# Token-major products that read each block of weights as two alternating streams

## The chip, the cores and the metric

The kernel runs on one core of one Trainium2 chip. The metric is the device time of one execution in microseconds; the weights are laid out on the host before the launch, which is not part of it.

## The reference

One layer of a decoder on 256 tokens with 2048 features, all in float32: a feed-forward block, a mixer of two gated branches, and a second feed-forward block, each followed by a layer norm over a scaled residual. Cut to what matters:

```python
h = layer_norm(DN_ALPHA * h + 0.5 * swiglu(h, ffn1_w_in[l], ffn1_w_out[l]), ln1_g[l], ln1_b[l])
q, k, v, qi, ki, wi, rx, rg, gates = split_cols(h @ w_in[l])
y_attn = dsa_attention(q, k, v, qi, ki, wi)
y_rnn = rglru_branch(rx, rg, conv_w[l], ...)
g_attn, g_rnn = jnp.split(jax.nn.sigmoid(gates), 2, axis=-1)
merged = g_attn * (y_attn @ w_attn_branch[l]) + g_rnn * (y_rnn @ w_rnn_branch[l])
h = layer_norm(DN_ALPHA * h + merged @ w_out[l], ln2_g[l], ln2_b[l])
h = layer_norm(DN_ALPHA * h + 0.5 * swiglu(h, ffn2_w_in[l], ffn2_w_out[l]), ln3_g[l], ln3_b[l])
```

`swiglu` is `(silu(a) * b) @ w_out` with `a, b` the halves of `h @ w_in`; its inner width is 5632. The weights are some 520 MB that are read once, and nearly all of the arithmetic is in products of the 256 tokens with them.

## The kernel before

**Products in three parts.** TensorE multiplies in a rounded float32 format (`float32r`). To keep precision, every operand is split into a rounded part h and a remainder l, and a product is three matmuls: h·h, h·l and l·h. For weights the split is done on the chip, piece by piece: ACT writes h (line 294, `hl`), then DVE writes l = w - h (line 295). A piece has up to 1024 columns; five split pieces can be held at a time (`HL_BUFS = 5`), and the class `Weights` loads and splits a few pieces ahead of the one in use. Some pieces of the feed-forward's second matrix are split by ACT and a DMA that adds (tiles `wd`).

**Token-major products.** In most products the activations are the stationary operand (128 features by 128 tokens, loaded by each matmul) and the weights are the moving one, in runs of 512 or 256 columns; the result lies in PSUM with tokens on partitions. These go through `three` (lines 766, 767 and 768, one for each part) and, at the start of a block behind a norm, through lines 793 and 795 in `eager`. The 512-column form is used for plain blocks of weights (`tokens`), the 256-column form for fast products: for some blocks seven products of 2 by 2 sub-blocks take the place of eight. They need sums of weight blocks, which DVE makes (`operand`, lines 249 to 256, each on blocks of 256 columns), and which are then split like other pieces.

**Feature-major products.** The recurrent branch and the index keys use weights as the stationary operand and 256 tokens as the moving one (`mm3`, lines 1415 to 1417; `mmB`, lines 756 and 757). They are not touched.

**Order.** PE, SP and POOL run in the order in which the code is written. The order of the work is set by a list of pieces and by plans written out by hand; ACT and DVE are ordered by a scheduler. In the time of the profile, the first feed-forward block runs to about 650 us, the mixer to about 1620, and the second feed-forward block from there to the end.

**Layout on the host.** `_layout` puts every weight matrix into blocks as the kernel loads them: `f_in` and `f_out` for the feed-forward, `a_blocks` for all other token-major products, `b_blocks` for the feature-major ones.

Of the kernel before, what the change touches and what calls it, by code (L numbers as in the profile page):

```python
# [15 lines left out]
P = 128  # L16
S = 256
D = 2048
FF = 5632
NK = D // P  # L20
NKF = FF // P
NBK = NKF // 2
# [366 lines left out]
def tile_layer(ctx, tc, x_fm, x_tm, pos, f1a, f1o, wA, wki, wB, wG, lru, wab, wrb, wo, f2a, f2o,  # L389
# [6 lines left out]
    V, A, T, G = nc.vector, nc.scalar, nc.tensor, nc.gpsimd  # L396
# [21 lines left out]
    def MM():  # L418
        return psum.tile([P, 512], F32, name=name("mm"), tag="mm", bufs=4)
# [65 lines left out]
    for i in range(NR + LAG):  # L485
# [4 lines left out]
        if i >= LAG:  # L490
            g, c = divmod(i - LAG, TPG)
            o = sum(LRU_COLS[:c])
# [266 lines left out]
    def blockB(x):  # L759
# [2 lines left out]
            mmB(ps, x[k], W.unit(P), k == 0, k == len(x) - 1)  # L762
        return ps

    def three(ps, xh, xl, w, start, stop):
        T.matmul(ps, xh, w[0], start=start, stop=False)  # L766
        T.matmul(ps, xh, w[1], start=False, stop=False)  # L767
        T.matmul(ps, xl, w[0], start=False, stop=stop)  # L768

    def tokens(ps, x, t, w, start, stop):  # L770
        three(ps, x[:, 0, t * P:(t + 1) * P], x[:, 1, t * P:(t + 1) * P], w, start, stop)

    def eager(hs, ps):


        ln, hs.halves = hs.halves, None
        behind = ln.behind
        base = W.cur + 1
        W.limit, W.cap = base + AHEAD - 1, len(W.pieces)
        with tc.issue_after(ln.normed):  # L780
            W.split_to(W.limit)
        ws = []
        for k in range(0, 8, 2):
            if k == 2:
                with tc.issue_after(behind[0]), tc.issue_after(behind[1]):
                    W.split_to(base + AHEAD)
            if k == 6:
                ln.half(1)
            ws += [W.unit(512) for _ in range(2)]
            for a in range(2):  # L790
                for j in (k, k + 1):
                    x = ln.first[j][:, a, :P]
                    T.matmul(ps[0], x, ws[j][0], start=j == 0 and a == 0, stop=False)
                    if a == 0:
                        T.matmul(ps[0], x, ws[j][1], start=False, stop=False)
        for k in range(8):
            tokens(ps[1], hs[k], 1, ws[k], k == 0, False)
            if k % 2:
                W.split_to(base + AHEAD + 1 + k // 2)
        W.limit = None  # L800

    def blockF(x, forms, plan, fill):
# [10 lines left out]
        if getattr(x, "halves", None):  # L813
            c = [MM(), MM()]
            eager(x, c)
            skip = 4
        for i, (form, k) in enumerate(plan):
# [26 lines left out]
            def run(ps, ops, start, stop):  # L844
                for r in range(2):
                    three(ps, *ops[r], W.unit(S), start and r == 0, stop and r == 1)
# [14 lines left out]
    def blockA(x, finish=None, lag=0, ln=None):  # L861
# [10 lines left out]
        if getattr(x, "halves", None):  # L872
            eager(x, ps)
            k = 8
# [677 lines left out]
    for j in range(-1, NR + LAG):  # L1552
# [15 lines left out]
        if j >= LAG:  # L1568
            i = j - LAG
            g, c = divmod(i, TPG)  # L1570
            xg = xcs[g * TPG:(g + 1) * TPG] if c else None
            if c == 1:
                open_heads = [BP() for _ in range(4)]
                ws = [W.unit(P) for _ in range(2)]
                for m in range(2):
                    for wi_, xi in ((0, 0), (0, 1), (1, 0)):
                        for b in range(4):
                            rows = slice(b * TAIL, (b + 1) * TAIL)
                            T.matmul(open_heads[b][:, m * S:(m + 1) * S], ws[m][wi_][rows], xg[0][rows, xi],
                                     start=m == 0 and wi_ == 0 and xi == 0, stop=False)  # L1580
            if c:
                ps = open_heads[c - 1]
# [3 lines left out]
            if c == TPG - 1:  # L1586
                ps = MM()
# [31 lines left out]
    for nb in range(4):  # L1619
# [3 lines left out]
        g, a = got  # L1623
# [19 lines left out]
def _layout(x, positions, ffn1_w_in, ffn1_w_out, ln1_g, ln1_b, w_in, conv_w, conv_b, lru_wa, lru_ba,  # L1643
            lru_wx, lru_bx, lru_lambda, w_attn_branch, w_rnn_branch, w_out, ln2_g, ln2_b, ffn2_w_in,
            ffn2_w_out, ln3_g, ln3_b):
    import numpy as np

    def c(a):
        return np.ascontiguousarray(a)

    def f_in(w):
        return c(w.reshape(NK, P, 2, NBK, 256).transpose(3, 1, 0, 2, 4)).reshape(NBK, P, NK * 512)

    def f_out(w):
        return c(w.reshape(NKF, P, 4, 512).transpose(2, 1, 0, 3)).reshape(4, P, NKF * 512)

    def a_blocks(w):
        n = w.shape[1] // 512
        nk = w.shape[0] // P
        return c(w.reshape(nk, P, n, 512).transpose(2, 1, 0, 3)).reshape(n, P, nk * 512)  # L1660

    def b_blocks(w):
        nk, n = w.shape[0] // P, w.shape[1] // P
        v = w.reshape(nk, P, n, P).transpose(2, 0, 1, 3).reshape(nk * n // 16, 16, P, P)
        return c(v.transpose(0, 2, 1, 3)).reshape(nk * n // 16, P, 2048)

    order = np.concatenate([np.concatenate([g * 640 + n * 160 + np.arange(HEAD, HEAD + TAIL) for n in range(4)]
                                           + [g * 640 + n * 160 + np.arange(HEAD) for n in range(4)])
                            for g in range(GRP)])
    w = w_in[0]  # L1670
    rx, rg = w[:, 4176:6736][:, order], w[:, 6736:9296][:, order]
    ki = np.zeros((D, P), w.dtype)
    ki[:, :80] = w[:, 4096:4176]

    lr = []
    for g in range(GRP):
        both = [[wm[g * 4 + n] for n in range(4)] for wm in (lru_wa[0], lru_wx[0])]
        u = [np.concatenate([wm[n][HEAD:, :HEAD] for n in range(4)], 0) for wm in both]
        for n in range(4):
            u += [wm[n][:HEAD, :HEAD] for wm in both]  # L1680
        for wm in both:
            tail = np.zeros((TPG, P, P), w.dtype)
            for n in range(4):
                c0 = n * TAIL
                tail[0, c0:c0 + TAIL, c0:c0 + TAIL] = wm[n][HEAD:, HEAD:]
                tail[1 + n, :, c0:c0 + TAIL] = wm[n][:HEAD, HEAD:]
            u += list(tail)
        lr.append(np.stack(u, 1).reshape(P, -1))

    def pc(vec, n):  # L1690
        return vec.reshape(n, P).T

    cols = np.concatenate([pc(ln1_g[0], NK), pc(ln1_b[0], NK), pc(ln2_g[0], NK), pc(ln2_b[0], NK)]
                          + [pc(conv_w[0, k][order], NR) for k in range(4)]
                          + [pc(a[0][order], NR) for a in (conv_b, lru_ba, lru_bx, lru_lambda)], axis=1)
    return dict(
        x_fm=c(x[0].reshape(S, NK, P).transpose(2, 1, 0)).reshape(P, NK * S), x_tm=c(x[0]),
        pos=c(positions[0].reshape(2, P).T),
        f1a=f_in(ffn1_w_in[0]), f1o=f_out(ffn1_w_out[0]), wA=a_blocks(w[:, :4096]),
        wki=c(ki.reshape(NK, P, P).transpose(1, 0, 2)).reshape(P, 2048), wB=b_blocks(np.concatenate([rx, rg], 1)),  # L1700
        wG=a_blocks(w[:, 9296:]),
        lru=c(np.stack(lr)), wab=a_blocks(w_attn_branch[0]), wrb=a_blocks(w_rnn_branch[0][order]),
        wo=a_blocks(w_out[0]), f2a=f_in(ffn2_w_in[0]), f2o=f_out(ffn2_w_out[0]), cols_d=c(cols),
        ln1_g=c(ln1_g[0]), ln1_b=c(ln1_b[0]), ln2_g=c(ln2_g[0]), ln2_b=c(ln2_b[0]),
        ln3_g=c(ln3_g[0]), ln3_b=c(ln3_b[0]))
# [16 lines left out]
```

## Time and profile before

| | us |
|---|---|
| median of 3 runs | 2339.02 (2338.2 to 2341.13) |
| span of the profiled execution, first to last instruction | 2334.1 |
| PE busy | 2309.5 |
| DVE busy | 2180.3 |
| ACT busy | 1583.6 |
| POOL busy | 304.6 |

The profile gives the execution's span and not its time with what lies around it; the median of the runs is 4.9 us above the span. Matmul records overlap, since a matmul is pipelined with the next: the spacing of their starts is what a matmul costs, not the length of its record. `PEld` is the load of the stationary operand, which runs beside PE. A row of the timeline gives start, length, engine, line, operation, output tile <- input tiles, shapes and count; where a row has a count over one, its length is from the first start to the last end. DMA moves 559.57 MB at a mean of 240 GB/s, and the granted TensorE clock is 0.999 of full speed over the span.

### The profile page before, as it was taken

Reading aid. Unit: us, or ns where it says so; the run is one execution under the profiler, and the core shown is the slowest. Engines: PE = TensorE matmul, PEld = TensorE weight load, DVE = VectorE, ACT = ScalarE, POOL = GpSimd, SP = SyncE. Lnnn points to the kernel's source line nnn. Section 1 sums busy time; section 2 is a strip of 40 time slices with the busy share of each in tenths; the row PEclk is TensorE's granted clock in tenths of the full one; section 3 lists DMA queues with packets and bytes.
Section 4 is the critical chain, followed back from the end, with each engine's and each line's share of the span. In section 5 each row is a group of like instructions: output and inputs, shape, how many; then the busy total and the mean of one; then the engine's idle time right before and its main releaser. Section 6 shows DMA issues by size and latency. Waiting matters only on the chain.

```text
span 2334.1 us, 40566 instructions
## 1 busy us (share of the span) xinstructions
PE 2309.5 (99%) x15430; PEld 2109.1 (90%) x15430; DVE 2180.3 (93%) x3172; ACT 1583.6 (68%) x2345; POOL 304.6 (13%) x416
## 2 busy tenths in 40 slices
PE   8999999999999999999999999999999999999998
PEld 7899999999988999888899998888889999999997
DVE  7899999999999999879887888998999999999997
ACT  7667777777757656556557785555667777777763
POOL 1111222222210000000110001100111112222220
PEclk9999999999999999999999999999999999999999
DMA  9778899999976555554665558755787899999986
GB/s 337 242 218 261 267 269 269 275 275 269 265 230 211 187 192 211 186 189 154 244 239 194 199 184 324 241 199 191 242 272 223 258 271 275 275 266 272 268 232 212
DMA packets 149091, 559.57 MB, mean 240 GB/s; under 512 B 17408, under 2 KB 18048, under 8 KB 124448
## 3 DMA queue, kind: packets, MB, share of 16 engines
q1 hardware_dynamic: 100800, 455.00, 54.4%
q0 software_dynamic: 47952, 101.85, 21.1%
q8 instruction: 121, 1.98, 0.3%
q14 instruction: 74, 0.61, 0.1%
q10 hardware_dynamic: 144, 0.13, 0.0%
HBM read 519.69 MB, written 37.22 MB: 239 GB/s over the span
## 4 chain that ended last, share of the span: by engine, by line
PE 71%; DVE 19%; issue 4%; DMA 4%; ACT 2%; POOL 0%; SPq 0%; ACTq 0%; DVEq 0%; POOLq 0%
PE mm L766 15%; PE mm L767 15%; PE mm L768 15%; DVE hl L295 10%; PE bp L767 5%; PE bp L766 5%; PE bp L768 5%; PE mm L1415 2%; PE mm L1417 2%; PE mm L1416 2%; DVE ws L249 2%; ACT hl L294 2%; DVE rf L256 1%; DVE rf L253 1%; DMA raw<-f1o 1%
## 5 line engine op out<-in xcount | busy, mean ns | idle before, releaser
L294 ACT ACTIVATE hl<-rf 128x1024 fp32r<-128x1024 f32 x573 | 516.0, 913 | 292.4 <-PE mm L768 135.1
L295 DVE TENSOR_TENSOR hl<-rf,hl 128x1024 fp32r<-128x1024 f32 x573 | 593.6, 1041 | 13.4 <-ACT hl L294 11.3
L295 DVE TENSOR_TENSOR hl<-raw,hl 128x1024 fp32r<-128x1024 f32 (+2 forms) x378 | 445.8, 1192 | 64.5 <-ACT hl L294 63.4
L294 ACT ACTIVATE hl<-raw 128x1024 fp32r<-128x1024 f32 (+2 forms) x378 | 386.0, 1034 | 174.5 <-PE mm L768 84.5
L767 PE MATMUL bp<-hl,sh 128*128 128x256 f32 x1146 | 321.4, 280 | 2.8 <-DVE hl L295 2.8
L766 PE MATMUL bp<-hl,sh 128*128 128x256 f32 x1146 | 321.1, 280 | 0.0
L768 PE MATMUL bp<-hl,sl 128*128 128x256 f32 x1146 | 320.4, 280 | 0.0
L766 PE MATMUL mm<-hl,hs 128*128 128x512 f32 (+1 forms) x800 | 274.4, 343 | 3.6 <-ACT yd L1197 3.0
L767 PE MATMUL mm<-hl,hs 128*128 128x512 f32 (+1 forms) x800 | 268.4, 335 | 0.7 <-DVE hl L295 0.7
L768 PE MATMUL mm<-hl,hs 128*128 128x512 f32 (+1 forms) x800 | 267.9, 335 | 0.1
L295 DVE TENSOR_TENSOR hl<-ws,hl 128x1024 fp32r<-128x1024 f32 x191 | 233.1, 1220 | 10.1 <-ACT hl L294 10.0
L249 DVE TENSOR_TENSOR ws<-rf 128x1024 f32<-128x1024 f32 x191 | 233.4, 1222 | 8.6 <-DMA rf<-wrb 2.7
L294 ACT ACTIVATE hl<-ws 128x1024 fp32r<-128x1024 f32 x191 | 201.9, 1057 | 57.6 <-DVE ws L249 23.5
L767 PEld LDWEIGHTS bp<-hl,sh 128*128 128x128 f32 x1146 | 215.2, 188 | 5.9 <-DVE hl L295 4.6
L768 PEld LDWEIGHTS bp<-hl,sl 128*128 128x128 f32 x1146 | 218.2, 190 | 0.0
L766 PEld LDWEIGHTS bp<-hl,sh 128*128 128x128 f32 x1146 | 215.2, 188 | 1.3
L1415 PE MATMUL mm<-hs,hl 128*128 128x256 f32 x640 | 178.1, 278 | 0.0
L1417 PE MATMUL mm<-hs,hl 128*128 128x256 f32 x640 | 177.6, 278 | 0.0
L1416 PE MATMUL mm<-hs,hl 128*128 128x256 f32 x640 | 177.6, 277 | 0.0
L766 PEld LDWEIGHTS mm<-hl,hs 128*128 128x128 f32 x800 | 150.3, 188 | 21.0 <-ACT yd L1197 4.2
L768 PEld LDWEIGHTS mm<-hl,hs 128*128 128x128 f32 x800 | 151.1, 189 | 16.8 <-DVE hs L960 0.5
L767 PEld LDWEIGHTS mm<-hl,hs 128*128 128x128 f32 x800 | 150.4, 188 | 15.5 <-DVE hl L295 1.4
(360 smaller groups left out, 5994.3 us busy)
## 6 DMA issues: line engine op xcount, KB each, us to landing
rf<-f1a SPq DMA_DIRECT2D x75, 1024.0 KB, 7.5
rf<-f2a SPq DMA_DIRECT2D x75, 1024.0 KB, 6.9
raw<-f1o SPq DMA_DIRECT2D x88, 512.0 KB, 6.8
raw<-f2o SPq DMA_DIRECT2D x88, 512.0 KB, 6.7
raw<-wB SPq DMA_DIRECT2D x80, 512.0 KB, 4.7
raw<-wG SPq DMA_DIRECT2D x54, 512.0 KB, 4.4
wd<-f1o POOLq DMA_DIRECT2D x92, 256.0 KB, 9.1
wd<-f2o POOLq DMA_DIRECT2D x92, 256.0 KB, 8.7
```

The costliest lines, as they stand in the source:

```text
L249: v.tensor_tensor(t, b[:, 0:4:3], b[:, 1:2].to_broadcast([P, 2, 2, 256]), op=OP.add)
L253: v.tensor_tensor(b[:, 1], t[:, 1], b[:, 0], op=OP.add)
L256: v.tensor_tensor(b[:, 0], b[:, 1], b[:, 2], op=OP.add)
L294: nc.scalar.activation(hp, src, AF.Copy)
L295: self.last = nc.vector.tensor_tensor(lp, src, hp, op=OP.subtract)
L766: T.matmul(ps, xh, w[0], start=start, stop=False)
L767: T.matmul(ps, xh, w[1], start=False, stop=False)
L768: T.matmul(ps, xl, w[0], start=False, stop=stop)
L1415: T.matmul(ps[:, :S], w[0], x[:, 0], start=first, stop=False)
L1416: T.matmul(ps[:, :S], w[0], x[:, 1], start=False, stop=False)
L1417: T.matmul(ps[:, :S], w[1], x[:, 0], start=False, stop=last)
```

## The change

The host lays out each 256 columns of the token-major weights as the 128 even columns and then the 128 odd ones (`woven` in `_layout`). In the kernel, the moving operand of each token-major matmul is read by an access pattern that undoes this: it takes one column from the first half of the 256, one from the second half, and so on, the two 512 bytes apart. The result is written to PSUM in the order of the original columns, contiguously. With 512 columns, the pattern does one block of 256 after the other. The number and order of the instructions on every engine, the tiles and the DMAs are the same as before; on PE a few waits on its own semaphore are placed otherwise.

```diff
+    def woven(ps, w):
+
+        if ps.shape[1] == S:
+            return ps.rearrange("p (k e) -> p k e", e=2), w.rearrange("p (e k) -> p k e", e=2)
+        return (ps.rearrange("p (h k e) -> p h k e", h=2, e=2),
+                w.rearrange("p (h e k) -> p h k e", h=2, e=2))
+
+    def product_of(ps, x, w, start, stop):
+        o, m = woven(ps, w)
+        T.matmul(o, x, m, start=start, stop=stop)
+
     def three(ps, xh, xl, w, start, stop):
-        T.matmul(ps, xh, w[0], start=start, stop=False)
-        T.matmul(ps, xh, w[1], start=False, stop=False)
-        T.matmul(ps, xl, w[0], start=False, stop=stop)
+        product_of(ps, xh, w[0], start, False)
+        product_of(ps, xh, w[1], False, False)
+        product_of(ps, xl, w[0], False, stop)
...
                     x = ln.first[j][:, a, :P]
-                    T.matmul(ps[0], x, ws[j][0], start=j == 0 and a == 0, stop=False)
+                    product_of(ps[0], x, ws[j][0], j == 0 and a == 0, False)
                     if a == 0:
-                        T.matmul(ps[0], x, ws[j][1], start=False, stop=False)
+                        product_of(ps[0], x, ws[j][1], False, False)
...
+    def woven(w):
+        return w.reshape(w.shape[0], -1, P, 2).swapaxes(2, 3).reshape(w.shape)
+
     def f_in(w):
-        return c(w.reshape(NK, P, 2, NBK, 256).transpose(3, 1, 0, 2, 4)).reshape(NBK, P, NK * 512)
+        return c(woven(w).reshape(NK, P, 2, NBK, 256).transpose(3, 1, 0, 2, 4)).reshape(NBK, P, NK * 512)
...
```

`f_out` and `a_blocks` call `woven` in the same way; `b_blocks` does not.

More of the change, by code (lines that the diff above doesn't have):

```diff
@@ L1649, in c @@
         return np.ascontiguousarray(a)
+    def woven(w):
+        return w.reshape(w.shape[0], -1, P, 2).swapaxes(2, 3).reshape(w.shape)
     def f_in(w):
-        return c(w.reshape(NK, P, 2, NBK, 256).transpose(3, 1, 0, 2, 4)).reshape(NBK, P, NK * 512)
+        return c(woven(w).reshape(NK, P, 2, NBK, 256).transpose(3, 1, 0, 2, 4)).reshape(NBK, P, NK * 512)
     def f_out(w):
-        return c(w.reshape(NKF, P, 4, 512).transpose(2, 1, 0, 3)).reshape(4, P, NKF * 512)
+        return c(woven(w).reshape(NKF, P, 4, 512).transpose(2, 1, 0, 3)).reshape(4, P, NKF * 512)
     def a_blocks(w):
@@ L1659, in a_blocks @@
         nk = w.shape[0] // P
-        return c(w.reshape(nk, P, n, 512).transpose(2, 1, 0, 3)).reshape(n, P, nk * 512)
+        return c(woven(w).reshape(nk, P, n, 512).transpose(2, 1, 0, 3)).reshape(n, P, nk * 512)
     def b_blocks(w):
```

## The prediction

> **What bounds the kernel now.** I read the page's busy shares and the chain that ended last first, then what PE waited for, then the spacing of single matmuls in the timeline, and last the busy time of each engine by stage. The page:
>
> ```profile
> span 2334.1 us, 40566 instructions
> PE 2309.5 (99%) x15430; PEld 2109.1 (90%) x15430; DVE 2180.3 (93%) x3172; ACT 1583.6 (68%) x2345; POOL 304.6 (13%) x416
> PE 71%; DVE 19%; issue 4%; DMA 4%; ACT 2%; POOL 0%; SPq 0%; ACTq 0%; DVEq 0%; POOLq 0%
> ```
>
> PE is busy nearly all the time, DVE not far behind. A busy PE says little, since matmul records overlap, so the second view is what PE waited for, longest first, the first and the last of its ten rows:
>
> ```profile
> PE mm L766 <- ACT hl L294: 5.6, 1, 5.6
> PE bp L767 <- DVE hl L295: 3.7, 9, 0.9
> ...
> PE bp L951 <- DVE y L971: 0.2, 1, 0.2
> ```
>
> No row is over 5.6 us, so ten rows are under 40 us of 2334 (they add to 19). The kernel is a stream of matmuls that hardly pauses; the time is the number of matmuls times their spacing. [...] In the timeline of PE, first the three-product groups (h·h, h·l, l·h: lines 766 to 768) on 512 columns, then on 256 columns, then the feature-major products of line 1415 to 1417, which also read 256 columns and load a new stationary tile each time:
>
> ```profile
> 319.74 0.39 PE L766 MATMUL mm<-hl,g 128*128 128x512 f32 x1
> ...
> 322.24 0.39 PE L768 MATMUL mm<-hl,g 128*128 128x512 f32 x1
> 1200.23 0.28 PE L766 MATMUL mm<-hl,ya 128*128 128x256 f32 x1
> ...
> 1201.53 0.28 PE L768 MATMUL bp<-hl,sl 128*128 128x256 f32 x1
> 1259.95 0.28 PE L1417 MATMUL mm<-hs,hl 128*128 128x256 f32 x1
> ...
> 1261.54 0.28 PE L1416 MATMUL mm<-hs,hl 128*128 128x256 f32 x1
> ```
>
> There are 11 steps between the first two rows: 2.50 / 11 = 0.227 us for 512 columns. Between the next two, 11 steps: 1.30 / 11 = 0.118 us for 256 columns. Between the last two, 14 steps: 1.59 / 14 = 0.1136 us for 256 columns. So equal shapes run at two spacings, 0.118 and 0.1136, and 512 columns cost a little less than two times 256. What could the array do if its operand came without a hitch? The nearest rows are products and transposes in plain float32:
>
> ```profile
> 1018.60 0.59 PE L1406 MATMUL bp<-pT,stg 128*128 128x256 f32 x2
> L1406 PE MATMUL bp<-pT,stg x32: 377/377/382, 1018.6 to 1096.3; 128*128 128x256 f32 x32
> 46.77 0.60 PE L1174 MATMUL bp<-ident,z 128*128 128x128 f32 x4
> L1174 PE MATMUL bp<-ident,z x176: 270/272/329, 46.8 to 2293.2; 128*128 128x128 f32 x176
> ```
>
> Two records of 0.377 in 0.59 start 0.59 - 0.377 = 0.213 us apart for 256 columns; four of 0.272 in 0.60 start (0.60 - 0.272) / 3 = 0.109 us apart for 128 columns. Both are 0.83 to 0.85 ns a column, twice 0.42. If a column can be taken in half that time, as the 0.227 suggests, that is about 0.216 us for 512 columns (the mean of 2 x 0.109 and 0.213) and 0.109 for 256. The products of interest take 0.227 and 0.118: 11 and 9 ns each that the array doesn't need. I find that excess only where 4-byte columns are taken at the higher rate, so it points at the read of the moving operand, alone or against the weight load that runs beside it. This is the stretch that the change touches.
>
> **The change, part by part.** Nothing is added or removed on any engine: instruction order, tiles, bytes and semaphores stay; each weight element lies elsewhere within its 256 columns, and the moving operand of the token-major products steps half a block (512 bytes) between one column and the next. PSUM is still written column by column. The sums that feed the fast products (L249, L253, L256) and the splits (L294, L295) act element by element on blocks of 256, so they cost the same. The DMAs move the same bytes in the same pieces: nothing. An access pattern with more dimensions needn't cost: on DVE a split from a tile read in separate runs and one read in one run take the same:
>
> ```profile
> L295 DVE TENSOR_TENSOR hl<-rf,hl 128x1024 fp32r<-128x1024 f32 x382 | 464.9, 1219 | 13.1 <-ACT hl L294 11.1
> L295 DVE TENSOR_TENSOR hl<-raw,hl 128x1024 fp32r<-128x1024 f32 x361 | 436.2, 1220 | 61.0 <-ACT hl L294 60.1
> ```
>
> What is left is the spacing of the token-major products, which no row of this trace shows with an alternating read: all moving operands here are contiguous. I bound it from both sides. From below: 0.216 and 0.109 us, as above. From above: a column every two cycles, 0.213 for 256 columns as L1406 does it, and 0.426 for 512. Between these I take 0.216 for 512 columns and 0.1136 for 256. The reason is the pair of rows at 0.118 and 0.1136: same shape, same loads, yet the one pays 4 ns more. So part of the excess depends on where the operands lie, not on the amount of work, and a read that spends twice as long on each address range (two streams share the time) can shift it. For 256 columns I don't go below 0.1136 as the likely value: no product of this kind runs faster in the trace.
>
> How many, and where? One of the three lines stands for each of them, as each has 4178 matmuls; the table is line 767 by stage, with its busy time and count, then all engines in the same stages:
>
> ```profile
> core 0: us, PE busy (x) PEld busy (x), PEclk, DMA share, GB/s
> 0.00:100.00 100.00, 56.63 (x158) 30.20 (x158) 1.00 0.88 303
> 100.00:650.00 550.00, 383.61 (x1257) 235.93 (x1256) 1.00 0.88 260
> 650.00:950.00 300.00, 140.93 (x444) 83.48 (x444) 1.00 0.60 207
> 950.00:1200.00 250.00, 137.20 (x399) 74.76 (x398) 1.00 0.57 197
> 1200.00:1370.00 170.00, 1.40 (x5) 0.82 (x5) 1.00 0.62 205
> 1370.00:1620.00 250.00, 143.59 (x408) 76.79 (x409) 1.00 0.67 235
> 1620.00:1710.00 90.00, 46.58 (x129) 24.05 (x128) 1.00 0.76 247
> 1710.00:2270.00 560.00, 392.09 (x1285) 241.24 (x1285) 1.00 0.89 260
> 2270.00:2334.00 64.00, 33.35 (x97) 18.21 (x97) 0.98 0.62 206
> sum 2334.00, PE 1335.40 PEld 785.48; mean PE 148.38 PEld 87.28
> core 0: us, PE busy (x) PEld busy (x) DVE busy (x) ACT busy (x) POOL busy (x), PEclk, DMA share, GB/s
> 0.00:100.00 100.00, 94.10 (x485) 80.08 (x486) 82.07 (x130) 68.57 (x106) 11.90 (x39) 1.00 0.88 303
> 100.00:650.00 550.00, 544.69 (x3843) 508.40 (x3842) 542.06 (x659) 410.78 (x593) 109.16 (x124) 1.00 0.88 260
> 650.00:950.00 300.00, 298.58 (x2084) 275.15 (x2083) 291.17 (x562) 182.54 (x269) 10.54 (x18) 1.00 0.60 207
> 950.00:1200.00 250.00, 250.00 (x1412) 217.35 (x1410) 219.02 (x376) 147.10 (x235) 13.97 (x26) 1.00 0.57 197
> 1370.00:1620.00 250.00, 249.53 (x1381) 217.71 (x1380) 231.89 (x346) 142.97 (x188) 19.79 (x37) 1.00 0.67 235
> 1620.00:1710.00 90.00, 87.67 (x451) 73.70 (x450) 81.71 (x146) 60.80 (x111) 12.85 (x21) 1.00 0.76 247
> 1710.00:2270.00 560.00, 556.81 (x3931) 519.40 (x3930) 554.10 (x673) 418.58 (x604) 111.74 (x128) 1.00 0.89 260
> 2270.00:2334.00 64.00, 58.08 (x308) 48.37 (x306) 47.94 (x69) 24.48 (x31) 10.36 (x17) 0.98 0.62 206
> ```
>
> Busy over count is the mean record, and with 0.39 us for 512 columns and 0.28 for 256 it gives the mix: in 100 to 650 us 383.61 / 1257 = 0.305, so 77% have 256 columns. Times three lines: 3771 products, about 840 wide and 2930 narrow. What PE offers there is 840 x 11 ns + 2930 x 4 ns = 9 + 12 = 21 us. But DVE, the third busy column, is free for only 550 - 542.1 = 7.9 us in this stage, and PE's weights come from its splits: it cannot deliver them sooner than it can work. I take the smaller of offer and room in each stage:
>
> - 0 to 100: offer 4, room 18: 4.
> - 100 to 650: offer 21, room 7.9: 7.9.
> - 650 to 950 (67% narrow): offer 8.4, room 8.8: 8.4.
> - 950 to 1200 (42%): offer 9.6, room 31: 9.6.
> - 1200 to 1370 has 5 of these products a line: 0.
> - 1370 to 1620 (35%): offer 10.5, room 18: 10.5.
> - 1620 to 1710: offer 3.5, room 8.3: 3.5.
> - 1710 to 2270 (78%): offer 21, room 5.9: 5.9.
> - 2270 on (42%): offer 2.3, room 16: 2.3.
>
> The offer is 81 us, of which 52 arrive. The profiled span of 2334.1 becomes 2282; the median of the runs, 2339.0, lies 4.9 above the span, and I leave that as it is: 2287 us. What is late next is the DVE split in the two feed-forward stages. With the lower bounds (11 and 9 ns) the same sum gives about 60 us: 2279. DVE's room may be too small, as its records overlap: two adjacent splits start closer together than one lasts. If half the rest of the offer in the two feed-forward stages then got through, some 25 us more: about 2255.
>
> **The rivals.** *The read gets slower.* If the operand's reader keeps one short line of SBUF and serves two or more neighbouring columns from it, alternating streams would miss on every column. The trace neither shows nor excludes it, because every moving operand is contiguous. Its price by the L1406 rows is a column every two cycles: 0.426 - 0.227 = 0.199 us on a wide product and 0.213 - 0.118 = 0.095 on a narrow one. Over all stages the mix is 1335.4 / 4178 = 0.320, 64% narrow: 8020 narrow and 4510 wide, so 762 + 897 = 1660 us, all on the path since PE is the bound: about 4000 us. It decides as soon as a product becomes slower at all: 1 ns more on each of 12,534 is 12.5 us. For it speaks that the excess of today shows a reader without slack at the full rate; against it that contiguous columns already pay, so the reader is not simply a line that is reused. [...]
>
> *Nothing changes.* The excess could belong to the weight load or to its handover: each product loads 128 columns, and 0.1136 against 0.118 may be a matter of the stationary operand's address, which stays. Then 2339. For it: 256-column products at 0.1136 exist with a contiguous read; against it: the wide products, whose load fills only half their time, have 11 ns too.
>
> *PE speeds up and the rest doesn't follow at all*: DVE and ACT wait for each other in rings of five buffers, and a smaller share arrives: with half of 52, 2313. That is within the first case.
>
> **How the numbers follow.** Faster as worked out: 0.67, at 2287, its own range 2250 to 2330. No change in the spacing: 0.13, at 2339. Slower read: 0.20, nearly all of it far out near 4000. The range of 2250 to 2345 holds the first two and leaves out the third. A change of 0.2% (4.7 us) is about what can be told from none here, and with it the chances are 0.67, 0.13 and 0.20.
>
> **What would show it.** Right: 512-column products of the three lines start 0.216 us apart and narrow ones 0.114 or less; DVE's busy share rises to 95%, its part of the chain that ended last grows, and PE's waits for the split at L295 in the feed-forward stages grow from a few us to tens. Lines 1415 to 1417 and 1200 to 1370 us stay as they are. Wrong: an unchanged 0.227; or 0.43, with DVE and ACT half idle. It would also be wrong if PE got faster and DMA, 0.88 busy in the feed-forward stages, then kept the splits waiting.

## The result and the profile after

The changed kernel takes 2317.34 us (median of 4 runs, 2313.93 to 2322.61) against 2338.61 before (2338.04 to 2341.13): a ratio of 0.9911, 95% interval 0.9896 to 0.9925. It is faster by 21 us, where 52 were forecast. The page after, in the rows shown of before:

```profile
span 2315.4 us, 40575 instructions
PE 2242.9 (97%) x15430; PEld 2081.5 (90%) x15430; DVE 2177.0 (94%) x3172; ACT 1577.1 (68%) x2345; POOL 307.3 (13%) x416
DVE 41%; PE 30%; issue 12%; DMA 8%; ACT 7%; POOL 1%; SPq 0%; ACTq 0%; DVEq 0%; POOLq 0%
```

PE's part of the chain that ended last fell from 71% to 30%, and DVE's rose from 19% to 41%: the bound has moved. All three lines of the product are now one line, 774. Its spacing in the timeline: 12 narrow products from the first row below to the second, then 21 wide ones in one row.

```profile
314.12 0.39 PE L774 MATMUL bp<-hl,sh 128*128 128x256 f32 x2
...
315.46 0.28 PE L774 MATMUL mm<-hl,xs 128*128 128x256 f32 x1
1373.64 4.70 PE L774 MATMUL mm<-hl,hs 128*128 128x512 f32 x21
```

Narrow: 1.34 / 12 = 0.112 us instead of 0.118. Wide: the row lasts 4.70 with a record of 0.38 at its end, (4.70 - 0.38) / 20 = 0.216 us instead of 0.227. So the read did what was forecast, to the nanosecond for the wide products and a little more for the narrow ones. Over the kernel, the narrow spacing of before had a median of 0.117, so PE's offer is 4512 x 11 ns + 8070 x 5.3 ns = 92 us. The span lost 18.7. What took the rest? PE's busy time fell by 67 us, but its idle time rose from 25 to 73 (span less busy time). PE's waits, longest first, before 5.6 and 3.7 us at the head:

```profile
PE mm L774 <- DVE hl L295: 25.5, 41, 1.9
PE mm L774 <- DVE z L1173: 9.6, 6, 3.2
PE bp L774 <- DVE hl L295: 8.3, 15, 0.9
```

The two layer norms inside the kernel are good landmarks, as their transposes (line 951 before, 962 after) are PE's first work behind the first feed-forward and its last before the second. First and last start of these, and of the last matmuls of the kernel, before and then after:

```profile
L951 PE MATMUL bp<-ident,y x32: 270/272/331, 703.1 to 1628.6; 128*128 128x128 f32 x32
L1052 PE MATMUL bp<-y,dg x6: 379/592/697, 2326.3 to 2328.4; 128*128 128x512 f32 x4, 128*128 128x256 f32 x2
L962 PE MATMUL bp<-ident,y x32: 272/273/327, 704.7 to 1613.0; 128*128 128x128 f32 x32
L1063 PE MATMUL bp<-y,dg x6: 379/592/697, 2307.7 to 2309.7; 128*128 128x512 f32 x4, 128*128 128x256 f32 x2
```

The first feed-forward so runs to 703 us in the kernel before, not to 650 as the section on that kernel has it, and the prediction's stage from 650 to 950 begins with its last 53 us. The first feed-forward became 1.6 us longer (703.1 to 704.7). The mixer gained 925.5 - 908.3 = 17.2 us, the second feed-forward 697.7 - 694.7 = 3.0. The two feed-forwards, where most of the products stand, gave 1.4 us together.

### The profile page after: what moved, and what is told of

It reads as the page before. It is cut to its first block, busy times and chain, and to the rows that moved or that the text cites. A ratio compares the mean times of both kernels' runs of the same rounds, so it can differ in the third digit from the quotient of the medians.

```text
span 2315.4 us, 40575 instructions
## 1 busy us (share of the span) xinstructions
PE 2242.9 (97%) x15430; PEld 2081.5 (90%) x15430; DVE 2177.0 (94%) x3172; ACT 1577.1 (68%) x2345; POOL 307.3 (13%) x416
## 4 chain that ended last, share of the span: by engine, by line
DVE 41%; PE 30%; issue 12%; DMA 8%; ACT 7%; POOL 1%; SPq 0%; ACTq 0%; DVEq 0%; POOLq 0%
DVE hl L295 22%; PE mm L774 16%; DVE ws L249 4%; PE bp L774 4%; ACT hl L294 4%; PE mm L1426 3%; DVE rf L253 3%; PE mm L1428 3%; PE mm L1427 3%; DVE rf L256 2%; DMA wd<-f1o 2%; DMA ya<-yd 1%; DVE z L1173 1%; ACT wd L199 1%; ACT wd L194 1%
## 5 line engine op out<-in xcount | busy, mean ns | idle before, releaser
L774 PE MATMUL mm<-hl,hs 128*128 128x512 f32 (+1 forms) x2448 | 461.2, 333 | 19.6 <-DVE hl L295 10.1
L774 PEld LDWEIGHTS mm<-hl,hs 128*128 128x128 f32 x2448 | 384.1, 191 | 61.2 <-DVE hl L295 13.7
L774 PE MATMUL bp<-hl,sh 128*128 128x256 f32 x2292 | 412.5, 277 | 8.0 <-DVE hl L295 7.4
L774 PEld LDWEIGHTS bp<-hl,sh 128*128 128x128 f32 x2292 | 353.1, 192 | 15.3 <-DVE hl L295 12.0
L774 PE MATMUL mm<-wd,g 128*128 128x512 f32 x1176 | 266.6, 379 | 2.1 <-DMA wd<-f1o 1.3
L774 PEld LDWEIGHTS mm<-wd,g 128*128 128x128 f32 x1176 | 218.3, 189 | 34.3 <-DMA wd<-f1o 3.6
L774 PE MATMUL mm<-hl,xs 128*128 128x256 f32 (+1 forms) x1212 | 203.5, 308 | 18.7 <-DVE hl L295 9.8
L774 PE MATMUL mm<-hl,g 128*128 128x512 f32 (+1 forms) x936 | 214.2, 382 | 6.2 <-DVE z L1173 5.5
L774 PEld LDWEIGHTS mm<-hl,xs 128*128 128x128 f32 x1212 | 173.1, 192 | 33.1 <-DVE hl L295 14.4
L774 PEld LDWEIGHTS mm<-hl,g 128*128 128x128 f32 x936 | 174.8, 192 | 30.6 <-issue 6.2
```

What stands on the lines that cost most here:

```text
L774: T.matmul(o, x, m, start=start, stop=stop)
```

## The experiments

**What the alternating read does, measured alone.** Two kernels that leave out the whole layer: groups of 48 matmuls on PE, nothing beside them, each with its own stationary load. In each, the line of a group is its pattern.

```python
T.matmul(ps, x(i), w(512), ...)                                              # contiguous
T.matmul(ps.rearrange("p (k e) -> p k e", e=2), x(i),
         w(512).rearrange("p (e k) -> p k e", e=2), ...)                     # two streams
T.matmul(ps.rearrange("p (e k) -> p e k", e=2), x(i),
         w(512).rearrange("p (k e) -> p e k", e=2), ...)                     # one stream, step of 2
```

> A kernel that computes nothing of the layer: 17 groups of 48 matmuls on PE alone, float32r, each with its own load of 128 stationary columns, no other engine at work. Each group reads its moving operand in another order. It measures the spacing by itself. Theory 'pairs' (neighbouring columns, first and second of a pair, are fetched on separate paths, each of which does best with its own contiguous run): contiguous 0.227 us for 512 columns, two streams 0.216 at any distance (1024, 512, 64 and 16 bytes), four or eight streams slower, since each path then jumps. Theory 'ranges' (a stall where the moving read and the weight load are in the same 64-byte range parity; two streams make the read dwell twice as long): 0.216 at 512 and 1024 bytes apart, 0.227 again at 64 and 16 bytes, four streams as good as two, and contiguous reads change with 64 bytes of offset. Theory 'lines' (columns of one short line must follow each other): two streams at no distance could be faster than contiguous, and steps of 4 or 16 columns take 0.43. For 256 columns: contiguous 0.113 to 0.120 by offset, two streams 0.109 to 0.112.

One row for each group; the spacing is (length - last record) / 47. The last record is 0.38 to 0.4 us for 512 columns in the quick groups, up to 0.69 in the slow ones, and 0.28 for 256 columns. In this order: contiguous; two streams 512, 1024, 64 and 16 bytes apart; four streams; eight; one stream with a step of 2, of 4, of 16 columns; contiguous from an address 64 bytes on; then 256 columns contiguous, contiguous from 64 bytes on, and in two streams; last, 512 contiguous columns with a load of half the stationary columns:

```profile
25.23 11.04 PE L60 MATMUL b<-mv,st 128*128 128x512 f32 x48
36.11 10.52 PE L64 MATMUL b<-mv,st 128*128 128x512 f32 x48
46.47 10.52 PE L68 MATMUL b<-mv,st 128*128 128x512 f32 x48
56.83 10.52 PE L72 MATMUL b<-mv,st 128*128 128x512 f32 x48
67.19 10.52 PE L76 MATMUL b<-mv,st 128*128 128x512 f32 x48
77.55 13.75 PE L80 MATMUL b<-mv,st 128*128 128x512 f32 x48
91.13 23.56 PE L84 MATMUL b<-mv,st 128*128 128x512 f32 x48
114.48 21.86 PE L88 MATMUL b<-mv,st 128*128 128x512 f32 x48
136.16 22.32 PE L92 MATMUL b<-mv,st 128*128 128x512 f32 x48
158.31 20.98 PE L96 MATMUL b<-mv,st 128*128 128x512 f32 x48
179.11 11.17 PE L100 MATMUL b<-mv,st 128*128 128x512 f32 x48
190.11 5.92 PE L104 MATMUL b<-mv,st 128*128 128x256 f32 x48
195.87 5.82 PE L108 MATMUL b<-mv,st 128*128 128x256 f32 x48
201.52 5.52 PE L112 MATMUL b<-mv,st 128*128 128x256 f32 x48
217.60 11.20 PE L124 MATMUL b<-mv,st 128*64 128x512 f32 x48
```

Contiguous 0.227; two streams 0.216 at every distance, 16 bytes included; four streams 0.283, eight 0.487; steps of 2, 4 and 16 take 0.452, 0.461 and 0.433. With 256 columns 0.120 and 0.112. "Ranges" is out as the cause of the gain (64 and 16 bytes are as good as 512), and so is a reader with one short line for all columns. What "ranges" expected of the address is there, though, and small: 64 bytes on, contiguous reads take 0.229 instead of 0.227 and 0.118 instead of 0.120, while two more groups of 256 columns in two streams at other addresses take 0.112 again. Why is open. With half the stationary columns loaded the spacing is 0.230: the excess of the contiguous read didn't shrink with the load. The idea of two fetch paths, one for each column of a pair, fits most of this. A second kernel tried what it says of patterns that were not in the first.

> A second kernel that only measures spacing on PE: 11 groups of 48 float32r matmuls, nothing of the layer. After the first one theory 'pairs' reads: the first and the second column of each pair are fetched on two paths; each path wants at least two of its columns from one 16-byte line, has a small loss at exactly two and none at four. It expects for 512 columns: contiguous 0.227, two streams 0.216, two streams each with a step of 2 columns 0.227 (two hits a line on each path), with a step of 4 columns 0.43 to 0.46 (one hit), each column read twice running 0.216, two columns of one stream and then two of the other 0.283 (each path jumps between streams, as with four streams), four and four 0.227. Theory 'one line at a time' (all columns of a line must follow each other) expects two and two better than two streams, and a step of 2 in two streams as slow as in one (0.451). Theory 'load' for narrow products: with two streams 0.1117 at 256 columns is more than half of 0.2158, so a load of 128 columns would be the bound there: at 384 columns 0.162, and at 128 columns contiguous and two streams both near 0.11.

In this order: two streams, each with a step of 2; each with a step of 4; each column twice running; two columns of one stream and two of the other; four and four; then 384 columns contiguous and in two streams; 128 contiguous and in two streams:

```profile
46.48 11.08 PE L68 MATMUL b<-mv,st 128*128 128x512 f32 x48
57.40 21.91 PE L72 MATMUL b<-mv,st 128*128 128x512 f32 x48
79.13 10.54 PE L76 MATMUL b<-mv,st 128*128 128x512 f32 x48
89.51 16.16 PE L80 MATMUL b<-mv,st 128*128 128x512 f32 x48
105.50 12.19 PE L84 MATMUL b<-mv,st 128*128 128x512 f32 x48
117.52 8.48 PE L88 MATMUL b<-mv,st 128*128 128x384 f32 x48
125.85 7.96 PE L92 MATMUL b<-mv,st 128*128 128x384 f32 x48
133.65 5.47 PE L96 MATMUL b<-mv,st 128*128 128x128 f32 x48
138.95 5.52 PE L100 MATMUL b<-mv,st 128*128 128x128 f32 x48
```

0.227, 0.453, 0.216: as expected of pairs, and a step of 2 in two streams is twice as fast as in one (0.452), which none of the theories of a single path named here gives. Two and two took 0.333 where 0.283 was expected, four and four 0.250 instead of 0.227: the order is right, the sizes are not, so what a jump costs on a path stays open. 384 columns take 0.162 in two streams against 0.173. At 128 columns the contiguous read takes 0.111 and two streams 0.112, as much as 256 columns in two streams: a product with its own load of 128 columns went no lower here. Whether the load sets this floor is open: no group with a smaller load and few columns was measured.

**Is it DVE that kept the offer?** First the kernels that leave DVE less to do by leaving work out: l of the pieces of fast products isn't computed, h stands in for it.

```diff
-                self.last = nc.vector.tensor_tensor(lp, src, hp, op=OP.subtract)
-            self.hl[self.split] = (h, l)
+                if not form:
+                    self.last = nc.vector.tensor_tensor(lp, src, hp, op=OP.subtract)
+            self.hl[self.split] = (h, h if form else l)
```

> The kernel before, without the DVE split of the pieces of fast products (their h stands in for l): DVE loses about 4 us of work per fast chunk, PE does the same matmuls. All theories: PE still bounds it, within 0.3% of 2339, a little less where DVE had been late (some 10 us).

> The changed kernel with the same splits left out. PE's offer by the measured spacings is 4512 x 11 ns + 8070 x 5.3 ns = 92 us. Theory 'DVE sets the pace of the feed-forward stages in the changed kernel': most of the offer arrives now, 75 to 92 us less than before_light, and a feed-forward block takes 29.4 us instead of 30.8. Theory 'transfers set the pace': the DMAs are all there, so a block stays at 30.6 to 30.8 and about 20 us arrive, as without the omission. Theory 'edges and clock': blocks at 29.4, but waits of 3 us with a lower granted clock behind them at the ends of the feed-forwards stay, and 60 to 75 us arrive.

Before 2325.80 us, changed 2260.49: 65 us apart, where the full kernels are 21 apart. (The kernel before gains 13 us itself, about what was expected.) The transposes of the gates (four to a block) give the length of a feed-forward block: first and last start of 24 or 20 of them, thus of six or five blocks, less 0.33 within a group, by five or four steps. Full kernels before and after, then light ones before and after, whose lines stand one further on:

```profile
L1174 PE MATMUL bp<-ident,z x24: 272/272/273, 331.4 to 486.3; 128*128 128x128 f32 x24
L1185 PE MATMUL bp<-ident,z x24: 272/273/273, 359.9 to 514.1; 128*128 128x128 f32 x24
L1175 PE MATMUL bp<-ident,z x20: 272/272/273, 230.9 to 354.8; 128*128 128x128 f32 x20
L1186 PE MATMUL bp<-ident,z x20: 272/272/273, 223.9 to 342.5; 128*128 128x128 f32 x20
```

30.9 and 30.8 us in full; 30.9 and 29.6 with DVE relieved. So the block's 1.3 us that PE offers are all there once DVE has room, and DVE allowed 0.1 of them. In blocks, the theory of DVE's pace came out; in all, 65 us is below the 75 to 92 that it expected and within the 60 to 75 of "edges and clock". About 44 of the 92 us come back with DVE's work left out. They include what DVE does to the loads: a split that ends sooner frees its buffer for a load sooner. Of the remaining 27, some are waits for transfers, which were smaller in the full kernel (0.6 and 1.3 us); the rows of PE's waits in the light changed kernel:

```profile
PE mm L775 <- DMA wd<-f2o: 9.0, 9, 1.9
PE mm L775 <- DMA wd<-f1o: 4.8, 3, 2.4
```

**Less work for DVE without leaving any out.** A feed-forward block has four chunks, and a chunk is fast where seven products take the place of eight. A fast chunk saves PE 0.5 us and costs DVE 4 (estimates from the spacings and the records of DVE). Three instead of four in the 16 blocks of each feed-forward that had four, in both kernels:

```diff
-FOUR = tuple(range(6, 22))
+FOUR = ()
```

> The changed kernel with three instead of four fast chunks in the 16 feed-forward blocks that had four (32 blocks in both feed-forwards). A fast chunk saves PE 24 wide minus 42 narrow products (5.18 - 4.70 = 0.5 us at the new spacings) and costs DVE about 4.0 us more (sums 1.13 + 0.6 + 0.6, splits 3.97 instead of 2.27). Theory 'DVE bounds the feed-forward stages, so PE's offer was lost there': PE becomes the bound again at some 29.9 us a block where it now takes 30.8: 32 x 0.9 = 29 us less, about 2288. Theory 'the weight transfers set the pace' (DMA is 0.89 busy there): no change, 2317. Theory 'waits and clock at the edges between stages took the gain, PE bounds the stages': 32 x 0.5 = 16 us more, 2333.

> The kernel before with the same three fast chunks: the control. PE bounded its feed-forward stages, so all theories but that of the transfers expect 32 x (24 x 0.227 - 42 x 0.1175 = 0.51) = 16 us more, about 2355; the transfers' theory expects 2339.

Before with three: 2364.58 us (1.0111, 1.0097 to 1.0125), 26 more, not 16. Changed with three: 2325.01 (0.9934, 0.9920 to 0.9947). The change is worth 40 us here instead of 21, as DVE's room would have it, but the kernel did not become faster: 2288 had been expected of DVE alone, and neither of the other two times, 2317 and 2333, came out. Where nothing stalls, its blocks take the 30.0 us of PE; PE waits elsewhere, in the changed kernel and, for less, in the one before:

```profile
PE mm L774 <- DVE z L1173: 28.4, 20, 4.7
PE mm L766 <- DVE z L1162: 10.8, 6, 4.5
```

The second wait was 2.4 us with four chunks; the 8 us more are most of the 10 that the control took over its forecast. PE's clock was lower as well: a mean of 0.993 to 0.996 in the runs of the changed kernel with three, against 0.998 to 1.000 for the kernel before; 0.5% of 2325 us would be some 12 us, by estimate. The sums of the gate (z, through which PSUM comes free) stand in DVE's queue behind work that waits for loads. From the waits of DVE and ACT in the changed kernel with three:

```profile
DVE ws L249 <- DMA rf<-f1a: 21.9, 13, 4.0
ACT wd L194 <- DMA raw<-f1o: 31.7, 17, 5.6
```

Two variants with fewer blocks of three fell short as well:

> The changed kernel with three fast chunks in the last two blocks of each feed-forward (four stay in the 14 before). In the changed kernel's trace the step from the 21st to the 22nd block's transposes takes 37.7 us in the first feed-forward and 33.9 in the second, in after_three 30.6 both times: a raw piece is loaded late because DVE frees its buffer late, and PE then waits 3.2 us and runs on at a lower clock. Theory 'the end of the stage is lost to DVE's lag': 7 + 3 us less than the changed kernel, about 2307. Theory 'the late load has its own cause': 2317 or, by PE's extra work, 2319.

> The changed kernel with four and three fast chunks in turn (four in blocks 7, 9, ... 19, three in the others). After_three's blocks took 30.0 us where nothing stalled, but PE waited 28 us for the sums of the gate (z) behind late loads. Theory 'DVE bounds': DVE's mean load per block falls by 2 us and PE's rises by 0.25, so blocks of 29.8 to 30.2 us, 20 to 30 us less than the changed kernel: about 2292. If the stalls of after_three come with any block of three: 2310 to 2320.

2323.44 us (0.9931, 0.9918 to 0.9944) with three in the last two blocks, 2320.79 (0.9920, 0.9907 to 0.9933) with three and four in turn. The wait of 3.2 us at the end of the first feed-forward went, as expected of after_edge, but both lost elsewhere what they gained: PE's waits for the split of line 295 add to 28.6 and 30.0 us in them, where the changed kernel has 25.5. The hoped-for times, 2307 and 2292, are misses; the other branches, 2317 to 2319 and 2310 to 2320, lie nearer and were passed too. DVE's load alone doesn't settle the time; late loads come next.

**Late loads.** A raw piece is one that is loaded and not yet split. Two remedies: 12 pieces fewer in each feed-forward on the DMA that adds (ACT and DVE split them), and a fifth buffer for raw pieces.

```diff
-                if k in (2, 6) and (g or nb >= 2) or k == 4 and g >= 2:
+                if k in (2, 6) and (g or nb >= 2):
```
```diff
-U_BUFS = 53
+U_BUFS = 51
-RAW_BUFS = 4
+RAW_BUFS = 5
```

> after_three (three fast chunks in all feed-forward blocks) with 12 pieces fewer in each feed-forward on the adding DMA: they are split by ACT and DVE as others are (DVE +1.13 us each, 14 us a feed-forward, where it has 65 to 70 us of room; 24 DMAs of 256 KB less of 92). Theory 'in after_three the transfers are late, and the loads' share of the DMA engines (0.91) is why': the waits of ACT and DVE for raw and rf fall, PE's waits for z (28 us) with them, 2300 to 2310 against 2325. Theory 'the lag is in the order on ACT and DVE, not in the transfers': 2320 to 2330.

> after_three with a fifth buffer for raw pieces and a look-ahead that is the same in number (two buffers less of the pool of small tiles make the room). SP waits over 1100 us in all for a split to free a buffer, so loads start late. Theory 'late loads from too few buffers': 2300 to 2310 against 2325. Theory 'share of the DMA engines': little, 2318 to 2325. Theory 'order on ACT and DVE': 2325.

> The changed kernel with the fifth buffer for raw pieces. The wait of 3.2 us at the end of the first feed-forward goes back to a raw piece that landed 7.6 us after its buffer came free. Theory 'late loads': that wait and the low clock behind it go, 4 to 10 us less than the changed kernel, 2307 to 2313. Theory 'DVE sets the pace in the blocks': the blocks stay at 30.8 us, so no more than that. If neither: 2317.

All three help: 2297.46 us with three chunks and fewer adding DMAs (0.9828, 0.9811 to 0.9846), 2310.09 with three and the buffer (0.9879, 0.9864 to 0.9893), 2305.41 for the changed kernel with the buffer alone (0.9857, 0.9843 to 0.9870). In three_far the waits of DVE for rf in the feed-forwards are gone from the top of the list, PE's wait for z fell from 28.4 to 6.2, and the blocks run through. ACT's waits for raw pieces, which were to fall with them, did not (33.4 us for f1o, 31.7 with three alone). The remedy takes both transfers (559.5 to 546.9 MB) and work of ACT (1528.5 to 1507.1 us busy) away; which of the two brought DVE's loads in time isn't separated. With three and the buffer, PE's wait for z fell only to 24.1. With the buffer alone, the wait of 3.2 us at the end of the first feed-forward is gone and a block still takes 30.8 us, as the expectation had it for DVE's pace; the gain of 12 us is over the 4 to 10 expected. PE's wait, then the transposes as above, with three alone and with fewer adding DMAs:

```profile
PE mm L774 <- DVE z L1173: 6.2, 5, 1.9
L1185 PE MATMUL bp<-ident,z x24: 272/272/273, 329.6 to 487.9; 128*128 128x128 f32 x24
L1185 PE MATMUL bp<-ident,z x24: 272/273/273, 358.6 to 509.2; 128*128 128x128 f32 x24
```

31.6 and 30.0 us a block. The controls, the same remedies without the change:

> The kernel before with three fast chunks and 12 pieces fewer on the adding DMA: the control for three_far (2297). If the change's gain was held back by DVE and late loads, this control is bound by PE at the old spacings, with blocks of 31.5 us: 2350 to 2360, so the change is worth 53 to 63 us there instead of 21. If fewer adding DMAs are a gain of their own: below 2339.

> The kernel before with the fifth raw buffer: the control for after_raw5 (2305). If late loads cost only the changed kernel: 2335 to 2339, and the change is worth 30 us or more with that buffer. If the buffer is a gain by itself: 2327, and the change is worth 21 as it was.

2355.38 us (1.0073, 1.0059 to 1.0087) and 2338.04 (0.9995, 0.9986 to 1.0004), both as expected: neither makes the kernel before faster than it was. So what the change is worth depends on what stands around it: 21 us as it came, 33 with a fifth buffer, 40 with three chunks, 58 with three chunks and fewer adding DMAs. Late loads are not a matter of the faster PE alone: with three chunks, fewer adding DMAs take 9 us off the kernel before (2364.58 to 2355.38) and 28 off the changed one (2325.01 to 2297.46). They cost the kernel with the faster PE more. Three chunks with the fifth buffer have no control without the change.

**Both together.**

> The changed kernel with all three: three fast chunks, fewer adding DMAs, five raw buffers. Three_far's blocks from the 7th on take 30.0 us without exception, which is PE's bound, so the buffer can only help the first blocks, the ends and the mixer: if the late loads there are as in the changed kernel, 5 to 10 us less than three_far, 2288 to 2292; if three_far has none left, 2297.

> As three_far_raw5, with two instead of three fast chunks in six blocks of the mixer's first product (there DVE was 99% busy from 750 to 950 us, and the change gained nothing in that stretch). PE has 6 x 0.5 = 3 us more to do, DVE 6 x 4 = 24 us less and less preparation. If DVE bounds that stretch: 3 to 6 us less than three_far_raw5; if it is order and waits: 0 to 3 us more.

2284.01 us (0.9763, 0.9750 to 0.9776), better than the 2288 to 2292 expected, and 2281.84 (0.9753, 0.9739 to 0.9766) with one fast chunk less in six blocks of the mixer: the least time of all, 57 us under the kernel before and 36 under the changed one. These two have no control without the change, so they don't say what the change is worth. That last step alone is within the spread of the runs (2281.1 to 2285.2 and 2278.1 to 2282.4), so whether DVE bounds that stretch of the mixer stays open. The chain that ended last in three_far_raw5 is PE's again:

```profile
PE 71%; DVE 18%; issue 4%; DMA 3%; ACT 3%; POOL 0%; SPq 0%; DVEq 0%; ACTq 0%; POOLq 0%
```

## Why the prediction was right and wrong

- *The spacing*: right. 0.216 and 0.112 against 0.216 and 0.1136. The bound from below for narrow products, 0.109, was read from transposes, whose load is shorter (0.14 against 0.19 us a record); the products stop at 0.112. That the read of the moving operand was at fault was argued and has since been measured alone; the address ranges given as the reason for a gain are out, since 16 bytes do as well as 512. For narrow products the value was taken from the quickest contiguous rows, so that it came near is in part luck.
- *No work added or moved; lines 1415 to 1417 unchanged; DVE's part of the chain grows*: right.
- *The offer*: 81 forecast (its terms as printed add to 80), 92 by the spacings measured.
- *What arrives*: wrong, and this is the step that failed, "I take the smaller of offer and room in each stage": 52 us by that rule, 21 measured. Lining up the same 15,430 matmuls in both traces, the stages gave, forecast first: 4 and 3.2; 7.9 and 1.0; 8.4 and -3.1; 9.6 and 8.8; 0 and 0.9; 10.5 and 5.4; 3.5 and -1.7; 5.9 and 3.5; 2.3 and 0.7. Where DVE really had room (950 to 1200 us) the sum held. Elsewhere it failed in three ways. First, DVE's idle time of a feed-forward stage wasn't room: DVE waited for ACT's half of a split in it, and still did afterwards (7.7 us in 100 to 650 before, 7.3 after). Blocks went from 30.9 to 30.8 us, and in the light kernels, with DVE's work less, to 29.6. Second, a stage's mean hid slices with hardly any room: in 750 to 950 us DVE was busy for 198.2 of 200 us before and for 198.8 of 200 in the same stretch after, and 0.9 us were gained; 7.0 of the stage's 8.8 us of room stood in the 100 us before it. In 1370 to 1620, half of the 10.5 came, and PE waited 3.9 us for splits there. Third, the negative entries: waits that were not there or shorter before. The -3.1 of 650 to 950 is -3.8 in its first 50 us, the end of the first feed-forward.
- *The third rival*, "a smaller share arrives", 2313 with half of 52, came nearer than the forecast; it was counted as part of the first case. Its ring of DVE and ACT waits is part of what the runs show, the late loads are not in it.
- *The new waits* were named as a way to be wrong ("DMA ... kept the splits waiting") and were not priced. One of them in full, at the end of the first feed-forward: DVE's split frees a raw buffer at 654.9 us, SP issues the load at once and it lands 7.6 us later, ACT waits for it, DVE's split and the gate's sum stand behind, and PE waits 3.23 us:

```profile
654.93 3.73 SPq L235 DMA_DIRECT2D raw<-f1o  x4
662.64 1.06 ACT L294 ACTIVATE hl<-raw 128x1024 fp32r<-128x1024 f32 x1 [6.07 <-DMA raw<-f1o]
663.73 1.23 DVE L295 TENSOR_TENSOR hl<-raw,hl 128x1024 fp32r<-128x1024 f32 x1 [4.62 <-ACT hl L294]
666.45 8.29 PE L774 MATMUL mm<-hl,g 128*128 128x512 f32 x24 [3.23 <-DVE z L1173]
```

- *The rival "slower"*: a column in twice the time happens with a step of 2 and more in one stream (0.452 us for 512 columns) and with a step of 4 in two (0.453), but not with two contiguous streams (0.216). The reader that it assumes, with one short line for neighbouring columns, doesn't fit: in the changed kernel columns read one after the other lie some 512 bytes apart, and the read is faster than the contiguous one (0.216 against 0.227). Counted for every other column alone, most spacings go with the distance from one to the next: 4 bytes with two streams (0.216), 8 with contiguous columns and with two streams with a step of 2 (0.227), 16 with a single stream with a step of 2 (0.452) and with two streams with a step of 4 (0.453). The distance doesn't give the times of four streams (0.283) or of two and two (0.333), where every other column lies in another stream than the one before it. That there are two paths is inferred from the spacings, not seen.
- *DVE's share at 95%*: 94%. *PE's waits for the split rise to tens of us*: 34 in all, 27 of them in the two feed-forward stages, as said.

## What to carry to other kernels

A float32r matmul of 512 columns took 5% less time when neighbouring columns came from two contiguous streams, 16 to 1024 bytes apart (0.216 against 0.227 us); a layout on the host is enough. With a step of 2 inside each stream the gain was gone (0.227). When one engine gets faster, another's idle time isn't room for it until one has seen what that engine waits for in it: test it by taking work away, and look at slices as short as one block. A change to the bound is also the time to set the balance anew: here the same change was worth 21 us with the old balance and 58 with one that had been worse before.

## What the runs showed of the hardware

After the wait of 3.23 us above, 24 wide products took 8.29 us, (8.29 - 0.38) / 23 = 0.344 us each instead of 0.216, and the granted clock (third from the end in these rows) was 0.93 over 650 to 700 us:

```profile
650.00:700.00 50.00, 46.77 (x229) 40.93 (x229) 40.89 (x95) 23.49 (x31) 3.82 (x8) 0.93 0.72 230
700.00:750.00 50.00, 47.04 (x264) 41.01 (x264) 47.53 (x121) 34.64 (x72) 1.14 (x2) 1.00 0.59 200
```

Over 666 to 672 us alone the clock was 0.50, and the wide products there start 0.427 us apart (0.56 after the first). The 23 spacings cost 23 x 0.128 = 2.9 us on top of the wait, so the wait and the slow products behind it took about twice its length. Not every wait was followed by such products: PE waited 2.30 us at 702 us, in the second row, and the clock stayed at 1.00. The fastest run of the changed kernel had the highest mean clock and the slowest the lowest: 2313.93 us at 0.999, 2322.61 at 0.994.
